# Splitting words into high and low parts: one ScalarE copy and one VectorE subtraction at every place

## The chip, the core and the metric

The kernel runs on one core of one Trainium2 chip. The metric is the device time of one execution in microseconds (us), as the median over runs. The core's engines are TensorE (PE: matmuls, with its weight loads shown apart as PEld), VectorE (DVE), ScalarE (ACT), GpSimd (POOL) and SyncE (SP), which here issues the DMAs. Each engine works through its own list of instructions in order; semaphores tie the lists together.

## What is computed

Two layers of a mixer block over 1024 latent tokens and 256 context tokens, of width 1024. Cut to what matters here:

```python
for l in range(2):
    hx = rms_norm(x, norm_g[l]) * (1 + scale) + shift        # and hc for the context
    q, k, v, g_att, c_a, c_b, g_conv, f_u, g_four = split_cols(hx @ w_in[l])
    attn = windowed_attention(rope(q), rope(k), v, kc, vc, sink)   # blocks of 128, window +-128, + 256 context keys
    y_conv = silu(layer_norm(depthwise_conv31(c_a * sigmoid(c_b))))
    y_four = real(fft2(f_u)) @ w_four + b_four
    y = concat(attn * silu(g_att), y_conv * silu(g_conv), y_four * silu(g_four)) @ w_out[l]
    x = x + gate * y                                          # layer 0 also updates the context
return rms_norm(x, final_g)
```

## The kernel before

Data are fp32. For the large products each operand is kept as two words of a shorter type, a high part and a low part: `hi` is a copy of the raw fp32 words into that type, `lo` is `raw - hi`. A product is then three matmuls, hi times hi, hi times lo and lo times hi (`mm3`, L198 to L200). Whatever goes into such a product has to be split first: one copy and one subtraction for each tile.

The order of the work is set by a scheduler that places each engine's instructions by priority with a timeline of its own; the code is written in the order of priority. Each layer runs in stages: projections beside the Fourier and convolution branches; then attention, 128 queries and two heads to a step (`Attention.step`), four steps to a block; inside attention the matmuls of other work are put as filler for TensorE, first the remaining projections (gates), then the halves of the output projection (`Out.half`). Step i computes scores of its two heads (`score`, two PSUM tiles of two banks), VectorE adds the mask and takes the row's extreme (`score<-score,mask`), ScalarE does the exponential (`p<-score,st`, L925), VectorE forms the reciprocal of the sum, GpSimd divides (`p<-p,st`, L941). A step later TensorE transposes p (L955, PSUM tile `pt`), ScalarE copies the high part (`ph`, L960), VectorE subtracts (`pl<-pt,ph`); then TensorE multiplies with v (L969, tile `mm`).

Places that split, and with which engines before:

- `w_split` (tiles `wr`, `wh`, `wl`, 128x1024): weights of the next projection; ScalarE copy (L408), subtraction on VectorE, but on GpSimd (L409) while attention runs, when `holding[0]` is true.
- `Wout.split` (tiles `wor`, `hxh`, `hxl`, 128x512, 16 in a layer): weights of the output projection, raw tiles coming through six slots that are loaded again after each split. Even k: ScalarE copy and GpSimd subtraction. Odd k: both on VectorE, the copy as a CAST.
- `Out.prep_rest` and `Out.prep` (tiles `wr`, `wh`, `wl`, 128x512): the two halves of an output block's input. The rest half goes by `holding[0]`, the other half subtracts on VectorE.
- `keys`, `w_tile_short` and the Fourier tables: ScalarE and VectorE already.

`modulate` (L400) and `four_fold` (L681, L686, L690) have subtractions of their own on GpSimd, which do not go through `split`. VectorE's instructions all have line 57, that of a recording helper, so they are told apart by their tiles.

## Time and profile before

| | |
|---|---|
| median of 3 runs | 1176.14 us (1173.57 to 1181.28) |
| the profiled execution | 1175.1 us, span of its instructions 1172.9 us |
| PE busy | 1095.1 us (93% of the span) |
| DVE busy | 828.8 us (71%) |
| ACT busy | 541.5 us (46%) |
| POOL busy | 285.7 us (24%) |
| mean granted TensorE clock | 0.972 of full speed |

Busy time is the time in which at least one instruction of the engine is on its way. What matters is the idle time of TensorE, and at which of the stages it lies. Attention runs from about 262 to 610 us in layer 0 and from about 838 to 1140 us in layer 1; the weights of the output projection are split at about 425 to 500 us and 950 to 1025 us.

### The profile page before, as it was taken

The numbers are of one execution on the slowest core, as the hardware profiler recorded it, in microseconds if no ns is written. First come the engines' busy times: TensorE is split into PE (matmuls) and PEld (weight loads), VectorE is DVE, ScalarE is ACT, GpSimd is POOL, SyncE is SP. The second block draws the span as 40 slices with busy tenths as digits, with TensorE's granted clock in tenths as the row PEclk, the third lists the DMA queues.
The fourth block names the chain that finished last, engine by engine and source line by source line (L and its number), as shares of the span: only waits on it lengthen the run. The fifth ranks groups of instructions, "written<-read, shape, count | busy, mean of one in ns | idle before, by whom it ended". The sixth has DMA issues, their size and how long they took to land.

```text
span 1172.9 us, 17178 instructions
## 1 busy us (share of the span) xinstructions
PE 1095.1 (93%) x6165; PEld 923.6 (79%) x6165; DVE 828.8 (71%) x1702; ACT 541.5 (46%) x1195; POOL 285.7 (24%) x271
## 2 busy tenths in 40 slices
PE   5999999999999999899999999989889997999986
PEld 2688887778878988788888788868678886788865
DVE  4545998997776567767665269999566677577763
ACT  4442222215566555555557653222346555455551
POOL 1230000002222234344553220000131344234321
PEclk9999999999999999899999999999989997899989
DMA  9711238453322253336458423532423254433210
GB/s 333 230 61 55 90 111 235 149 193 81 86 87 75 79 161 98 97 113 205 161 191 269 141 60 107 169 114 72 108 63 86 91 149 127 116 108 91 91 54 36
DMA packets 150924, 144.90 MB, mean 124 GB/s; under 512 B 7302, under 2 KB 128566, under 8 KB 150840
## 3 DMA queue, kind: packets, MB, share of 16 engines
q1 hardware_dynamic: 150840, 143.82, 40.5%
q8 instruction: 48, 0.79, 0.3%
q14 instruction: 36, 0.29, 0.1%
HBM read 109.71 MB, written 34.09 MB: 123 GB/s over the span
## 4 chain that ended last, share of the span: by engine, by line
PE 73%; DVE 12%; DMA 7%; ACT 3%; issue 2%; SPq 2%; POOL 1%; DVEq 0%; ACTq 0%; POOLq 0%
PE mm L198 13%; PE mm L199 13%; PE mm L200 13%; PE mm L969 5%; PE pt L955 5%; PE pt L198 5%; PE pt L199 5%; PE pt L200 4%; PE score L899 2%; PE score L901 2%; DMA wr<-od 2%; DVE score L57 2%; DVE cy L57 2%; DMA wada<-w_ada 1%; DVE pl L57 1%
## 5 line engine op out<-in xcount | busy, mean ns | idle before, releaser
L198 PE MATMUL mm<-hxh,wh 128*128 128x512 f32 (+1 forms) x808 | 312.4, 388 | 8.5 <-DVE t L57 4.5
L199 PE MATMUL mm<-hxl,wh 128*128 128x512 f32 (+1 forms) x808 | 309.4, 383 | 0.0
L200 PE MATMUL mm<-hxh,wl 128*128 128x512 f32 (+1 forms) x808 | 308.4, 382 | 0.0
L198 PEld LDWEIGHTS mm<-hxh,wh 128*128 128x128 f32 x808 | 154.2, 192 | 39.1 <-DVE t L57 5.9
L57 DVE SCALAR_TENSOR_TENSOR cy<-cu,cw,cy 128x1009 f32<-128x1009 f32 (+25 forms) x180 | 175.7, 1005 | 0.9
L200 PEld LDWEIGHTS mm<-hxh,wl 128*128 128x128 f32 x808 | 154.2, 191 | 27.6
L199 PEld LDWEIGHTS mm<-hxl,wh 128*128 128x128 f32 x808 | 154.5, 191 | 25.3 <-issue 0.5
L941 POOL TENSOR_SCALAR p<-p,st 128x640 f32<-128x640 f32 (+2 forms) x144 | 109.2, 771 | 261.9 <-DVE st L57 162.8
L57 DVE TENSOR_TENSOR pl<-pt,ph 128x512 fp32r<-128x512 f32 x184 | 111.9, 616 | 70.1 <-ACT ph L960 68.3
L409 POOL TENSOR_TENSOR wl<-wr,wh 128x512 fp32r<-128x512 f32 (+1 forms) x31 | 56.3, 1817 | 392.2 <-ACT wh L408 388.6
L960 ACT ACTIVATE ph<-pt 128x512 fp32r<-128x512 f32 x184 | 97.4, 541 | 112.4 <-PE pt L955 109.5
L925 ACT ACTIVATE p<-score,st 128x640 f32<-128x640 f32 (+2 forms) x144 | 105.5, 735 | 37.8 <-DVE st L57 36.6
L57 DVE CUSTOM_DVE_ANT_0 score<-score,mask,nsink 128x640 f32<-128x640 f32 (+2 forms) x144 | 111.1, 782 | 13.9 <-PE score L901 9.8
L408 ACT ACTIVATE wh<-wr 128x1024 fp32r<-128x1024 f32 (+1 forms) x74 | 61.8, 850 | 119.1 <-PE mm L199 72.0
L955 PE MATMUL pt<-ident,p 128*128 128x128 f32 x640 | 105.2, 283 | 11.2 <-DVE pl L57 7.8
L198 PE MATMUL pt<-hxh,wh 128*128 128x512 f32 (+1 forms) x296 | 110.7, 378 | 1.1 <-ACT gsum L341 1.1
L199 PE MATMUL pt<-hxl,wh 128*128 128x512 f32 (+1 forms) x296 | 109.4, 370 | 0.3 <-POOL hxl L400 0.3
L200 PE MATMUL pt<-hxh,wl 128*128 128x512 f32 (+1 forms) x296 | 108.3, 366 | 0.0
L969 PE MATMUL mm<-ph,v 128*128 128x256 f32 x320 | 91.5, 311 | 5.4 <-ACT ph L960 3.7
L955 PEld LDWEIGHTS pt<-ident,p 128*128 128x128 f32 x640 | 79.3, 145 | 21.9 <-issue 7.7
L969 PE MATMUL mm<-pl,v 128*128 128x256 f32 x320 | 92.9, 313 | 3.7 <-DVE pl L57 3.7
L969 PEld LDWEIGHTS mm<-ph,v 128*128 128x128 f32 x320 | 64.2, 201 | 8.9 <-ACT ph L960 5.9
(230 smaller groups left out, 1795.5 us busy)
## 6 DMA issues: line engine op xcount, KB each, us to landing
wada<-w_ada SPq DMA_DIRECT2D x48, 512.0 KB, 7.3
wr<-w_in SPq DMA_DIRECT2D x38, 512.0 KB, 4.1
qq<-qd SPq DMA_DIRECT2D x36, 256.0 KB, 4.5
x1d<-x SPq DMA_DIRECT2D x10, 512.0 KB, 3.8
xnd<-xr SPq DMA_DIRECT2D x10, 512.0 KB, 3.7
p<-xnd SPq DMA_DIRECT2D x10, 512.0 KB, 4.9
sg<-sgd SPq DMA_DIRECT2D x36, 128.0 KB, 3.0
wr<-yd SPq DMA_DIRECT2D x18, 256.0 KB, 4.3
```

Source lines behind the costliest of these rows:

```text
L57: r = f(*args, **kw)
L198: T.matmul(o, lhsT=lhs[0], rhs=rhs[0], start=start, stop=False)
L199: T.matmul(o, lhsT=lhs[0], rhs=rhs[1], start=False, stop=False)
L200: T.matmul(o, lhsT=lhs[1], rhs=rhs[0], start=False, stop=stop)
L408: S.activation(hi, raw, AF.Copy)
L409: (E or (G if holding[0] else V)).tensor_tensor(out=lo, in0=raw, in1=f32(hi), op=ALU.subtract)
L899: T.matmul(sc[:, c0:512], lhsT=q2[:, h, :], rhs=kx[:, k0:k0 + nl], start=fst, stop=not fst)
L925: S.activation(pp[:, j * n:(j + 1) * n], z["sc"][j][:, 768 - n:768], AF.Exp, scale=-1.0, bias=st[:, j:j + 1], accum_out=st[:, 4 + j:5 + j])
L941: G.tensor_scalar(out=pp[:, j * n:(j + 1) * n], in0=pp[:, j * n:(j + 1) * n], scalar1=st[:, 6 + j:7 + j], scalar2=1.0, op0=ALU.mult, op1=A ...
L955: T.transpose(out=bt[:, (j % 2 * 2 + y) * P:(j % 2 * 2 + y + 1) * P], in_=pp[:, c0:c0 + P], identity=ident)
L960: S.activation(ph, bt[:, :w], AF.Copy)
L969: T.matmul(o, lhsT=self.vv[kt][:, kv * P:(kv + 1) * P], rhs=y.cols(j * 256, (j + 1) * 256), start=(j == 0 and x == 0), stop=(j == z["nkt"] ...
```

## The change

`split` loses its arguments for engines. At each place it is now one ScalarE copy for the high part and one VectorE subtraction for the low part, inside attention too.

```diff
-    def split(hi, lo, raw, E=None, by_vector=False):
-
-        if by_vector:
-            V.tensor_copy(out=hi, in_=raw)
-        else:
-            S.activation(hi, raw, AF.Copy)
-        (E or (G if holding[0] else V)).tensor_tensor(out=lo, in0=raw, in1=f32(hi), op=ALU.subtract)
+    def split(hi, lo, raw):
+
+        S.activation(hi, raw, AF.Copy)
+        V.tensor_tensor(out=lo, in0=raw, in1=f32(hi), op=ALU.subtract)
...
-            split(self.hi[k].lat[:, hs], self.lo[k].lat[:, hs], self.raw[h, k], V if k % 2 else G, k % 2 == 1)
+            split(self.hi[k].lat[:, hs], self.lo[k].lat[:, hs], self.raw[h, k])
...
-            split(yh[:, :512], yl[:, :512], raw[:, :512], V)
+            split(yh[:, :512], yl[:, :512], raw[:, :512])
...
-                    split(kh.cols(s0, s1), kl.cols(s0, s1), raw.cols(s0, s1), V)
+                    split(kh.cols(s0, s1), kl.cols(s0, s1), raw.cols(s0, s1))
```

The scheduler places the instructions anew, so rows around the splits move too. First place: VectorE in layer 1, at the first eight splits of the output projection's weights (`hxh_6158` to `hxh_6186` are the high parts for k = 0 to 7, `wor` the raw slots, `pl_9040` the low part of p that TensorE multiplies with v, `t_9110` an evacuation that frees an `mm` bank). Before:

```order
L57 TENSOR_TENSOR ot_8878<-t_9074,mm 64x256
L57 CAST hxh_6162<-wor_9112 128x512
L57 TENSOR_TENSOR hxl_6164<-wor_9112,hxh_6162 128x512
L57 CAST hxh_6170<-wor_9113 128x512
L57 TENSOR_TENSOR hxl_6172<-wor_9113,hxh_6170 128x512
L57 CAST hxh_6178<-wor_9114 128x512
L57 TENSOR_TENSOR pl_9040<-pt,ph_9038 128x256
L57 TENSOR_TENSOR hxl_6180<-wor_9114,hxh_6178 128x512
L57 CAST hxh_6186<-wor_9112 128x512
L57 ISA score,st<-score,mask,nsink 128x640
```

Now the same place reads:

```order
L57 TENSOR_TENSOR ot_8878<-t_9074,mm 64x256
L57 ISA score,st<-score,mask,nsink 128x640
L57 ISA st 128x1
L57 TENSOR_TENSOR hxl_6160<-wor_9112,hxh_6158 128x512
L57 TENSOR_TENSOR hxl_6164<-wor_9112,hxh_6162 128x512
L57 TENSOR_TENSOR hxl_6168<-wor_9113,hxh_6166 128x512
L57 TENSOR_TENSOR hxl_6172<-wor_9113,hxh_6170 128x512
L57 TENSOR_TENSOR hxl_6176<-wor_9114,hxh_6174 128x512
L57 TENSOR_TENSOR hxl_6180<-wor_9114,hxh_6178 128x512
L57 TENSOR_TENSOR pl_9040<-pt,ph_9038 128x256
```

The mask step of the second head (the ISA row on `score`) stood behind four casts and three subtractions and now stands ahead of six subtractions.

Second place: ScalarE at the same splits (`p_9126` are the exponentials of this step's two heads). Before:

```order
L981 ACTIVATE t_9074<-mm 64x256
L408 ACTIVATE hxh_6158<-wor_9112 128x512
L933 ACTIVATE st<-nsink,st 128x1
L408 ACTIVATE hxh_6166<-wor_9113 128x512
L408 ACTIVATE hxh_6174<-wor_9114 128x512
L960 ACTIVATE ph_9038<-pt 128x256
L925 ACTIVATE p_9126,st<-score,st 128x640
L408 ACTIVATE hxh_6182<-wor_9112 128x512
L518 ACTIVATE t_9110<-mm 128x512
L925 ACTIVATE p_9126,st<-score,st 128x640
```

Now (three lines less in the file, so L405 is the copy of L408, L957 that of L960 and L922 the exponential of L925):

```order
L978 ACTIVATE t_9074<-mm 64x256
L405 ACTIVATE hxh_6158<-wor_9112 128x512
L930 ACTIVATE st<-nsink,st 128x1
L405 ACTIVATE hxh_6162<-wor_9112 128x512
L405 ACTIVATE hxh_6166<-wor_9113 128x512
L405 ACTIVATE hxh_6170<-wor_9113 128x512
L405 ACTIVATE hxh_6174<-wor_9114 128x512
L930 ACTIVATE st<-nsink,st 128x1
L405 ACTIVATE hxh_6178<-wor_9114 128x512
L957 ACTIVATE ph_9038<-pt 128x256
L922 ACTIVATE p_9126,st<-score,st 128x640 x2
```

Six copies instead of three stand ahead of `ph` and the first exponential, and none is left between the two exponentials.

Third place: VectorE in layer 0, in the first half of attention, where `w_split` makes the weights of the next projection (`t_3731` is an evacuation that frees an `mm` bank):

```order
 L57 ISA st 128x1
+L57 TENSOR_TENSOR wl<-wr,wh 128x1024
 L57 SCALAR_TENSOR_TENSOR t_3731<-t_3731,mm 128x256
 L57 ISA score,st<-score,mask,nsink 128x640
 L57 ISA st 128x1
 L57 TENSOR_TENSOR pl_3662<-pt,ph_3660 128x256
+L57 ISA score,st<-score,mask,nsink 128x640
+L57 ISA st 128x1
 L57 TENSOR_TENSOR pl_3750<-pt,ph_3748 128x512
```

The subtraction over 1024 columns now stands on VectorE, ahead of a bank's evacuation and of a mask step.

## Rows read from the trace of the kernel before

**Rows 1.** Busy time by stretch: PE, PEld, DVE, ACT, POOL, then granted clock, DMA share, GB/s.

```profile
262.00:425.00 163.00, 158.56 (x972) 140.19 (x971) 112.77 (x246) 96.15 (x227) 44.53 (x43) 1.00 0.31 85
425.00:500.00 75.00, 65.23 (x385) 58.12 (x384) 57.81 (x113) 42.13 (x100) 27.06 (x25) 0.93 0.41 119
...
950.00:1025.00 75.00, 64.10 (x324) 55.34 (x323) 53.24 (x97) 35.31 (x80) 30.35 (x25) 0.86 0.45 131
1025.00:1130.00 105.00, 99.67 (x585) 86.63 (x583) 82.12 (x209) 62.48 (x152) 38.68 (x39) 1.00 0.29 89
```

**Rows 2.** Timeline of PE: instructions with idle time before them, and releaser.

```profile
437.83 0.38 PE L969 MATMUL mm<-ph,v 128*128 128x256 f32 x1 [2.02 <-ACT ph L960]
...
472.79 0.58 PE L198 MATMUL mm<-hxh,wh 128*128 128x256 f32 x1 [2.90 <-DVE t L57]
...
968.68 0.69 PE L899 MATMUL score<-kh,q 128*128 128x384 f32 x1 [2.98 <-ACT p L925]
...
993.03 1.09 PE L955 MATMUL pt<-ident,p 128*128 128x128 f32 x4 [3.78 <-DVE pl L57]
```

**Rows 3.** Timeline of ACT around two of those waits.

```profile
436.88 0.63 ACT L408 ACTIVATE hxh<-wor 128x512 fp32r<-128x512 f32 x1 [3.93 <-DMA wor<-w_out]
...
967.74 0.79 ACT L925 ACTIVATE p<-score,st 128x640 f32<-128x640 f32 x1 [4.53 <-DVE st L57]
```

**Rows 4.** Timeline of DVE, layer 1, splits of the output projection's weights.

```profile
959.69 1.17 DVE L57 TENSOR_TENSOR hxl<-wor,hxh 128x512 fp32r<-128x512 f32 x1
960.78 0.41 DVE L57 CAST hxh<-wor 128x512 fp32r<-128x512 f32 x1
...
962.24 1.51 DVE L57 CAST hxh<-wor 128x512 fp32r<-128x512 f32 x1
...
965.37 1.48 DVE L57 CAST hxh<-wor 128x512 fp32r<-128x512 f32 x1
...
968.85 0.16 DVE L57 TENSOR_TENSOR st<-st 128x2 f32<-128x2 f32 x1
968.92 0.68 DVE L57 SCALAR_TENSOR_TENSOR cy<-cy,t 128x512 f32<-128x512 f32 x1
...
980.08 1.22 DVE L57 TENSOR_TENSOR q<-qq,q 64x1024 fp32r<-64x1024 f32 x1
...
984.01 1.79 DVE L57 SCALAR_TENSOR_TENSOR cy<-cy,t 128x512 f32<-128x512 f32 x1
985.73 1.24 DVE L57 TENSOR_TENSOR st<-st 128x2 f32<-128x2 f32 x1
...
993.74 2.19 DVE L57 TENSOR_TENSOR q<-qq,q 64x1024 fp32r<-64x1024 f32 x1
```

**Rows 5.** Timeline of POOL at the same time.

```profile
961.75 4.82 POOL L409 TENSOR_TENSOR hxl<-wor,hxh 128x512 fp32r<-128x512 f32 x3
```

**Rows 6.** Timeline of DVE, layer 0, the same splits.

```profile
432.64 2.35 DVE L57 CAST hxh<-wor 128x512 fp32r<-128x512 f32 x2
...
466.95 1.85 DVE L57 CAST hxh<-wor 128x512 fp32r<-128x512 f32 x2
```

**Rows 7.** Groups of POOL instructions that the change removes.

```profile
L409 POOL TENSOR_TENSOR wl<-wr,wh 128x1024 fp32r<-128x1024 f32 x14 | 33.4, 2386 | 353.2 <-ACT wh L408 353.2
L409 POOL TENSOR_TENSOR hxl<-wor,hxh 128x512 fp32r<-128x512 f32 x16 | 23.7, 1496 | 22.4 <-ACT hxh L408 22.3
L409 POOL TENSOR_TENSOR wl<-wr,wh 128x512 fp32r<-128x512 f32 x17 | 22.9, 1349 | 39.0 <-ACT wh L408 35.4 <-DVE wl L57 3.6
```

**Rows 8.** Groups of DVE instructions of the same kinds.

```profile
L57 DVE CAST hxh<-wor 128x512 fp32r<-128x512 f32 x16 | 12.7, 804 | 1.1 <-DMA wor<-w_out 1.0
...
L57 DVE TENSOR_TENSOR dft<-dft,dfth 128x1024 fp32r<-128x1024 f32 x8 | 9.8, 1221 | 3.0 <-ACT dfth L408 3.0
...
L57 DVE TENSOR_TENSOR hxl<-t,hxh 128x512 fp32r<-128x512 f32 x12 | 8.3, 692 | 0.4
```

**Rows 9.** Group of ACT instructions that the change doubles.

```profile
L408 ACT ACTIVATE hxh<-wor 128x512 fp32r<-128x512 f32 x16 | 10.0, 627 | 11.1 <-DMA wor<-w_out 6.6 <-PE mm L200 4.5
```

## Prediction

> **What bounds the kernel now.** I read first the table of busy time by stretch. In the first half of layer 0's attention TensorE is busy 158.6 of 163 us and VectorE 112.8 (69%): TensorE sets the pace, the others have room. In the two stretches in which the output projection's weights are split it is otherwise: TensorE is busy 65.2 of 75 us and 64.1 of 75 us, idle for 9.8 and 10.9 us, and the granted clock falls to 0.93 and 0.86 of full speed, which by these means costs another 75 x 0.07 = 5.3 us and 75 x 0.14 = 10.5 us of speed [rows 1]. So these 150 us hold 20.7 us of idle time and 15.8 us of slowness; a change that touches the splits is decided here first.
>
> Then the timeline of TensorE in these stretches, for what ended each idle time. Four waits hold 11.7 of the 20.7 us: 2.02 us for the copy `ph`, 2.90 us for an evacuation `t` of a matmul bank by VectorE, 2.98 us for an exponential that frees a score bank, 3.78 us for a `pl` subtraction that frees a transpose bank [rows 2]. One step further back, on ScalarE: the exponential of the third had waited 4.53 us for VectorE's mask step, and the `ph` of the first stood behind a weight copy that had waited 3.93 us for its w_out DMA [rows 3]. And VectorE before that mask step: a CAST of 128x512 that takes 0.41 us at 960.78 takes 1.51 us at 962.24 and 1.48 us at 965.37 [rows 4]. At that time GpSimd runs three split subtractions in a row, 4.82 us from 961.75 on [rows 5]. The same shows on other kinds of instruction, each beside its own quick copy: 1.79 against 0.68 us (`cy`), 1.24 against 0.16 us (`st`), 2.19 against 1.22 us (`q`). Together these five rows lose 1.10 + 1.07 + 1.11 + 1.08 + 0.97 = 5.3 us on VectorE in 35 us [rows 4]. In layer 0 two pairs of casts take 2.35 and 1.85 us where 0.82 would do [rows 6]. A VectorE instruction that reads its data from SBUF waits while a GpSimd subtraction is on; that is how the stretch becomes VectorE's.
>
> **The change part by part.** GpSimd loses 14 + 16 + 17 = 47 subtractions, 33.4 + 23.7 + 22.9 = 80.0 us [rows 7]. It waited for others most of the time, so nothing of this is a gain by itself.
>
> VectorE gets these 47. At undisturbed speed a 1024-column one takes 1.22 us and a 512-column one 0.69 us [rows 8]: 14 x 1.22 = 17.1 us, and 33 x 0.69 = 22.8 us. It loses 16 casts, 12.7 us with their stretching [rows 8]. That is 27 us more. Against it stands the stretching of other instructions that ends: 1.11 + 1.08 + 0.97 = 3.2 us by the rows shown, the least it can be; I take about 10 us for the whole trace as an estimate from there, since two of the six stretches of attention hold the larger part. The new subtractions can themselves meet a divide on GpSimd, which stays: one that did took 1.17 us instead of 0.69 [rows 4]. GpSimd is busy 140.6 of 418 us in the four stretches, the leaving subtractions included [rows 1], so a sixth is a fair share: 47/6 x 0.48 = 4 us, at most 23 us if all did. In all VectorE's busy time grows by some 20 us (between 14 and 40).
>
> ScalarE gets 16 copies of 0.63 us, 10.0 us in all [rows 9]; it is busy 42 and 35 of the 75 us there [rows 1].
>
> What of this lies on the path, place by place:
>
> Layer 1, first eight splits. The second mask step now stands ahead of the subtractions, so the 4.53 us wait of the exponential ends. In its place six copies stand ahead of both exponentials: 6 x 0.63 = 3.8 us. Counted from 960 us, when the first copy began, with 0.3 for a sink exponential, 0.4 for `ph` and twice 0.79 for the exponentials, the second ends at about 966.1 instead of 968.5. Saved: 2.4 of the 2.98 us.
>
> Layer 1, second eight. Ahead of the awaited `pl` the stretched `cy` and `st` give back 1.11 + 1.08 = 2.2 us; more subtractions stand there now (six for three casts and three subtractions, 4.1 for 3.3 us), which takes 0.8. Saved: 1.4 of 3.78 us.
>
> Layer 0, first eight. The copies that wait for the refilled slots now stand behind the exponentials, so `ph` does not wait for that DMA: 2.0 us saved. Layer 0, second eight: the two casts ahead of the evacuation lose 1.0 us of stretching; saved 1.0 of 2.90.
>
> Clock. In layer 1 each us of idle goes with 10.5/10.9 = 0.96 us of slowness, in layer 0 with 5.3/9.8 = 0.54. I take half of that for the us saved: 3.8 x 0.48 + 3.0 x 0.27 = 2.6 us. So far -(3.8 + 3.0 + 2.6) = -9.4 us.
>
> Cost elsewhere. The fourteen long subtractions stand in the first half of attention, ahead of evacuations and mask steps. Between 0 (VectorE has 31% idle time) and all 17.1 us. TensorE lost 4.4 us there to 112.8 us of VectorE's work [rows 1], that is 0.04 us per us; at twice that, because the new instructions stand right ahead of what TensorE awaits, 17.1 x 0.08 = 1.4 us. The seventeen short ones run mostly beside the halves of the output projection, where VectorE is at 82.1 of 105 us and TensorE loses 5.3 [rows 1]: 17 x 0.69 x 0.13 = 1.5 us. Sum: 2.9 us. The next projection's weights are ready a whole chunk of matmuls before use, so a later `wl` is covered there; without that cover it would be up to 1.22 us a time.
>
> The total is -9.4 + 2.9 = -6.5 us on an execution of 1175.1 us (span 1172.9), which is 1168.6. The median of the runs is 1 us above that execution, so I forecast **1169 us**.
>
> [...]
>
> **The rivals.** *Bigger gain.* If the lock between the two engines is what makes most of the idle time in the two stretches, since each stretched instruction delays all that stands behind it in VectorE's list, two thirds of the 20.7 us and the same part of half the 15.8 us of slowness go: -13.8 - 5.3 = -19 us, with next to no cost elsewhere: 1156 us. For it: five rows within 35 us on one engine. Against: 9 of the 20.7 us of idle time lie outside the four waits read, and `pl` and mask steps read PSUM and show no stretching.
>
> *Nothing gained.* VectorE takes on 20 us; the waits keep their length because six subtractions in one piece (4.1 us) now hold up `pl`, where casts and subtractions held it up before. The 1.4 to 2.4 us savings shrink to half and the price elsewhere doubles: -4.7 + 5.8 = +1, 1177 us.
>
> *Slower.* ScalarE's copies in front of the exponentials become what TensorE waits for. The price is 16 x 0.63 = 10.0 us, and with it half of the slowness per us of idle, some 0.5 x 10: +15 us, nothing saved: 1190 us. It decides from the point at which a block of six copies (3.8 us) plus what follows is longer than the matmuls that TensorE has in hand, some 18 of 0.23 us; the 3.93 us wait for w_out [rows 3] shows how a copy can hold ScalarE, and sixteen more of them can. Against: ScalarE's share of 47 to 56% in these stretches.
>
> The Trainium skill (Perfetto Trace Analysis, "Optimizing Scalar/DVE Operations") speaks for that side in general: where VectorE is saturated, it says, moving work to ScalarE or even GpSimd may make sense, which is what the kernel did; by it the 20 us that return to an engine busy for 71 to 78% would cost. The same section adds that moving between VectorE and GpSimd might not help, for the shared port.
>
> That the change doesn't do what it says is no rival here: no split subtraction stands in GpSimd's list any more. The subtractions of `modulate` and `four_fold` stay there, outside attention.
>
> **How the numbers follow.** The forecast case (1162 to 1176) has 0.47, the bigger gain 0.15, nothing gained (1174 to 1182) 0.19, slower 0.19. Leaving out a tenth at either end gives 1155 to 1190. About 1% is what a measurement of this kernel can tell from no change: faster than 1164.4 has the bigger gain's 0.15 and the lower edge of the forecast, 0.27 with the doubt about how rows were placed anew; slower than 1187.9 has 0.18; the rest, 0.55, lies within 1%.
>
> **What would show it.** If I am right, casts are gone from VectorE, its `cy`, `st` and `q` in the two stretches keep to 0.68, 0.16 and 1.22 us, TensorE's idle time there falls from 20.7 to about 14 us and the clock of 950 to 1025 us rises above 0.9; TensorE's busy time in the first half of attention stays above 156 of 163 us. Wrong would be: waits of TensorE for exponentials or `ph` that stand behind runs of weight copies on ScalarE; or new idle time behind `t` and mask steps, right after a `wl` of 1.22 us. Since the scheduler placed all of attention anew, a shift of a few us away from any split is possible as well, and would make the sum wrong without touching its reasons.

## Result and the profile after

| | before | after |
|---|---|---|
| median of 4 runs (us) | 1174.86 | 1158.29 |
| lowest to highest (us) | 1171.57 to 1181.28 | 1153.87 to 1159.50 |
| the profiled execution, its span (us) | 1175.1, 1172.9 | 1158.92, 1157.0 |
| mean granted clock of that execution | 0.972 | 0.980 |

The ratio of after to before is 0.984 with a 95% interval of 0.9807 to 0.9873: 18.8 us less, with 14.9 and 22.7 us at the ends of the interval; the medians differ by 16.6 us. I had forecast 1169 us, a gain of 6.5. The time lies in my range of 1155 to 1190 us and in the direction forecast, but outside the forecast case (1162 to 1176 us): the size is that of the rival I called the bigger gain (1156 us), to which I gave a chance of 0.15. Two executions at a lower granted clock, one of the kernel before at 1190.6 us and one of e10 at 1366.0 us, are left out of every ratio in this document.

The page of after, busy time by engine:

```profile
PE 1085.4 (94%) x6165; PEld 913.8 (79%) x6165; DVE 832.1 (72%) x1733; ACT 551.1 (48%) x1211; POOL 212.1 (18%) x224
```

The same line of the page before:

```profile
PE 1095.1 (93%) x6165; PEld 923.6 (79%) x6165; DVE 828.8 (71%) x1702; ACT 541.5 (46%) x1195; POOL 285.7 (24%) x271
```

These two lines divide the gain. The span fell by 15.9 us. TensorE's idle time, the span less its busy time, went from 77.8 to 71.6 us: 6.2 of it. The other 9.7 us is busy time: the same 6165 matmuls, done at a mean granted clock of 0.980 instead of 0.972, which is 23.1 us of slowness (1157.0 x 0.020) instead of 32.8 (1172.9 x 0.028). And VectorE, which got 47 subtractions and lost 16 casts (31 instructions more), is busy only 3.3 us longer; I had forecast some 20, and 14 at the least. GpSimd lost 73.6 us.

The table of busy time by stretch, after, columns as in [rows 1]:

```profile
262.00:425.00 163.00, 157.72 (x977) 140.09 (x976) 115.71 (x255) 97.78 (x230) 27.31 (x34) 1.00 0.31 83
425.00:500.00 75.00, 68.82 (x423) 60.43 (x422) 57.22 (x123) 47.04 (x110) 20.63 (x20) 1.00 0.44 133
950.00:1025.00 75.00, 68.43 (x390) 59.77 (x389) 56.88 (x121) 47.87 (x110) 18.20 (x19) 0.98 0.46 135
1025.00:1130.00 105.00, 97.43 (x554) 85.00 (x554) 79.86 (x208) 58.03 (x140) 33.17 (x33) 0.93 0.27 83
```

Against [rows 1]: in the two stretches of the w_out splits TensorE is idle for 6.2 and 6.6 us instead of 9.8 and 10.9, 12.8 in all where I had said about 14, and the clock is 1.00 and 0.98 instead of 0.93 and 0.86. In the first half of attention TensorE is busy 157.7 of 163 us, where it was 158.6: 0.8 us more idle time.

These stretches are fixed in time, and after the change the program is ahead by 8 us in the second and by 15 in the last (table of steps below), so the later rows don't show the same work. The 0.93 of the last stretch is not a loss: the clock falls at the last steps of attention in both kernels, before behind the end of this stretch, after inside it. The slices of 25 us that hold this fall, before and then after:

```profile
1125.00:1150.00 25.00, 21.22 (x99) 17.55 (x98) 14.04 (x35) 9.15 (x22) 6.98 (x8) 0.80 0.09 32
```

```profile
1100.00:1125.00 25.00, 18.29 (x94) 15.53 (x94) 17.89 (x58) 16.39 (x42) 5.86 (x8) 0.73 0.15 54
```

That is 25 x 0.20 = 5.0 and 25 x 0.27 = 6.8 us of slowness, 1.8 us given back.

What ended TensorE's idle time in the two stretches, from its timeline after (start, duration, instruction, idle time before it and releaser; the first splits of layer 0, and every wait above 1 us of the two stretches):

```profile
432.68 0.50 PE L198 MATMUL mm<-hxh,wh 128*128 128x512 f32 x1 [0.50 <-DVE t L57]
...
470.14 0.39 PE L198 MATMUL mm<-hxh,wh 128*128 128x256 f32 x1 [1.75 <-DVE t L57]
...
481.20 0.44 PE L896 MATMUL score<-kh,q 128*128 128x384 f32 x1 [1.14 <-ACT p L922]
...
979.05 0.63 PE L952 MATMUL pt<-ident,p 128*128 128x128 f32 x4 [1.86 <-DVE pl L57]
982.54 0.44 PE L896 MATMUL score<-kh,q 128*128 128x384 f32 x1 [1.80 <-ACT p L922]
986.20 0.44 PE L952 MATMUL pt<-ident,p 128*128 128x128 f32 x2 [1.53 <-DVE pl L57]
988.27 0.50 PE L966 MATMUL mm<-pl,v 128*128 128x256 f32 x1 [1.17 <-DVE pl L57]
```

Of the four waits of [rows 2] those of 2.02 and 2.98 us are gone, that of 2.90 for an evacuation is 1.75 long and that of 3.78 for a `pl` 1.86. Layer 1 keeps four waits in a row at its second eight splits, 6.4 us together, and three of them end with a `pl` of VectorE.

One new wait lies just ahead of the second stretch. VectorE and then TensorE, after:

```profile
940.91 1.47 DVE L57 TENSOR_TENSOR wl<-wr,wh 128x1024 fp32r<-128x1024 f32 x1 [0.59 <-ACT wh L405]
```

```profile
943.84 0.50 PE L198 MATMUL mm<-hxh,wh 128*128 128x512 f32 x1 [1.71 <-DVE t L57]
```

A moved 1024-column subtraction, 1.47 us long beside a divide of GpSimd that runs from 940.51 to 943.05, stands ahead of a mask step and of the evacuation `t` for which TensorE waits. The same comes once more 20 us earlier (1.48 us, and a wait of 1.71 at 923.91).

VectorE at the first eight splits of layer 1, timeline after:

```profile
961.07 0.89 DVE L57 CUSTOM_DVE_ANT_0 score<-score,mask,nsink 128x640 f32<-128x640 f32 x1
961.88 0.14 DVE L57 DVE_READ_ACCUMULATOR2_ANT st<- 128x1 f32 x1
961.88 0.81 DVE L57 TENSOR_TENSOR hxl<-wor,hxh 128x512 fp32r<-128x512 f32 x1
962.60 0.68 DVE L57 SCALAR_TENSOR_TENSOR cy<-cy,t 128x512 f32<-128x512 f32 x1
...
990.28 0.13 DVE L57 TENSOR_TENSOR st<-st 128x2 f32<-128x2 f32 x1
```

No casts; `cy` takes 0.68 us, `st` 0.13, a split subtraction 0.81. Between 959 and 992 us these three kinds take at most 0.68, 0.16 and 0.81 us, where in [rows 4] they took up to 1.79, 1.24 and 1.17. Of the two `q` of this stretch one takes 1.22 us and one, beside a divide of GpSimd, 1.68.

ScalarE at the first eight splits of layer 0, timeline after:

```profile
433.69 0.64 ACT L405 ACTIVATE hxh<-wor 128x512 fp32r<-128x512 f32 x1 [1.78 <-PE mm L200]
...
435.32 1.66 ACT L405 ACTIVATE hxh<-wor 128x512 fp32r<-128x512 f32 x3
...
437.07 1.14 ACT L405 ACTIVATE hxh<-wor 128x512 fp32r<-128x512 f32 x2
438.24 0.39 ACT L957 ACTIVATE ph<-pt 128x256 fp32r<-128x256 f32 x1
438.52 0.79 ACT L922 ACTIVATE p<-score,st 128x640 f32<-128x640 f32 x1
```

Six copies stand ahead of `ph` and the exponential, and none waits for its DMA; before, the copy at 436.88 waited 3.93 us for it [rows 3].

**Where in the program the gain lies.** VectorE runs one RECIPROCAL of `st` for each of the 72 attention steps of the two layers, so its start tells where attention stands. From VectorE's timeline, in us:

| RECIPROCAL | before | after | difference |
|---|---|---|---|
| 1st (first step of layer 0) | 281.28 | 282.06 | +0.8 |
| 16th | 408.07 | 407.90 | -0.2 |
| 19th | 440.52 | 432.54 | -8.0 |
| 40th (last of layer 0) | 611.80 | 604.15 | -7.7 |
| 41st (first of layer 1) | 851.57 | 843.35 | -8.2 |
| 53rd | 958.48 | 951.35 | -7.1 |
| 55th | 988.63 | 970.53 | -18.1 |
| 58th | 1016.47 | 1001.46 | -15.0 |
| 72nd (last) | 1134.34 | 1119.26 | -15.1 |

Between the 16th and the 19th, the first w_out splits of layer 0, 7.8 us are gained and kept to the end of the layer. Between the 53rd and the 58th, those of layer 1, 7.9 are gained and kept to the 72nd. Elsewhere the two executions run side by side, to within some us: the scheduler put other matmuls between the steps, so that a single step moves by several us either way (the 22nd comes 0.9 us later than before, the 55th 18.1 us earlier).

### The profile page after: what moved, and what is told of

Its sections match the earlier page's. It is cut to its first block, busy times and chain, and to the rows that moved or that the text cites. A ratio compares the mean times of both kernels' runs of the same rounds, so it can differ in the third digit from the quotient of the medians.

```text
span 1157.0 us, 17196 instructions
## 1 busy us (share of the span) xinstructions
PE 1085.4 (94%) x6165; PEld 913.8 (79%) x6165; DVE 832.1 (72%) x1733; ACT 551.1 (48%) x1211; POOL 212.1 (18%) x224
## 4 chain that ended last, share of the span: by engine, by line
PE 78%; DVE 6%; DMA 6%; ACT 5%; issue 2%; SPq 1%; POOL 1%; ACTq 0%; DVEq 0%; POOLq 0%
PE mm L198 14%; PE mm L199 14%; PE mm L200 14%; PE pt L952 5%; PE mm L966 5%; PE pt L198 5%; PE pt L199 5%; PE pt L200 5%; PE score L896 3%; PE score L898 2%; DMA wada<-w_ada 2%; ACT p L922 2%; DVE cy L57 1%; DVE wl L57 1%; DVE score L57 1%
## 5 line engine op out<-in xcount | busy, mean ns | idle before, releaser
L938 POOL TENSOR_SCALAR p<-p,st 128x640 f32<-128x640 f32 (+2 forms) x144 | 115.1, 812 | 732.2 <-DVE st L57 380.8
L957 ACT ACTIVATE ph<-pt 128x512 fp32r<-128x512 f32 x184 | 97.5, 543 | 97.7 <-PE pt L952 96.8
L57 DVE CUSTOM_DVE_ANT_0 score<-score,mask,nsink 128x640 f32<-128x640 f32 (+2 forms) x144 | 111.0, 781 | 14.7 <-PE score L898 13.8
L922 ACT ACTIVATE p<-score,st 128x640 f32<-128x640 f32 (+2 forms) x144 | 105.3, 735 | 28.6 <-DVE st L57 27.5
L405 ACT ACTIVATE wh<-wr 128x1024 fp32r<-128x1024 f32 (+1 forms) x74 | 62.0, 851 | 116.4 <-PE mm L199 76.9
L57 DVE TENSOR_TENSOR wl<-wr,wh 128x1024 fp32r<-128x1024 f32 (+1 forms) x74 | 76.7, 1041 | 44.6 <-ACT wh L405 44.5
L966 PE MATMUL mm<-pl,v 128*128 128x256 f32 x320 | 89.7, 305 | 1.2 <-DVE pl L57 1.2
L966 PE MATMUL mm<-ph,v 128*128 128x256 f32 x320 | 88.5, 304 | 0.5 <-ACT ph L957 0.3
L198 PEld LDWEIGHTS pt<-hxh,wh 128*128 128x128 f32 x296 | 55.6, 190 | 14.2 <-issue 2.4
```

The costliest lines, as they stand in the source:

```text
L57: r = f(*args, **kw)
L198: T.matmul(o, lhsT=lhs[0], rhs=rhs[0], start=start, stop=False)
L405: S.activation(hi, raw, AF.Copy)
L922: S.activation(pp[:, j * n:(j + 1) * n], z["sc"][j][:, 768 - n:768], AF.Exp, scale=-1.0, bias=st[:, j:j + 1], accum_out=st[:, 4 + j:5 + j])
L938: G.tensor_scalar(out=pp[:, j * n:(j + 1) * n], in0=pp[:, j * n:(j + 1) * n], scalar1=st[:, 6 + j:7 + j], scalar2=1.0, op0=ALU.mult, op1=A ...
L957: S.activation(ph, bt[:, :w], AF.Copy)
```

## The experiments

Three accounts of the gain had to be told apart. *Stretching*: VectorE's instructions that read SBUF stand still while GpSimd subtracts, and all behind them is late. *Casts*: VectorE is freed of 16 casts, which ScalarE takes. *Start*: the weight splits of `w_split` and `prep_rest` change where the scheduler puts the first w_out copies, and with that a wait for a DMA ends. Ratios below are to the kernel before, with 95% intervals, and the us are the ratio's part of the kernel before's median of the same comparison (1175.23, 1174.71 and 1175.47 us). "Layer 0" and "layer 1" are the us, against before, from the 1st to the 40th and from the 41st to the 72nd RECIPROCAL of the one profiled execution; they time the steps of attention and not all work around them, so they need not add up to the gain. The expectations call the first account the lock theory, and the third first the order and then the start theory.

| kernel | ratio | us | layer 0 | layer 1 |
|---|---|---|---|---|
| the change | 0.9840 [0.9807, 0.9873] | -18.8 | -8.4 | -6.9 |
| e1_wout_only | 0.9913 [0.9880, 0.9947] | -10.2 | +4.1 | -8.7 |
| e2_rest_only | 0.9987 [0.9961, 1.0013] | -1.5 | -2.7 | -0.5 |
| e3_wout_casts_kept | 0.9947 [0.9923, 0.9971] | -6.2 | +9.5 | -9.6 |
| e4_wout_copies_act | 0.9963 [0.9931, 0.9995] | -4.3 | +5.2 | -6.9 |
| e5_prep_rest_too | 0.9935 [0.9915, 0.9956] | -7.6 | +1.5 | -5.1 |
| e6_w_split_too | 0.9932 [0.9904, 0.9960] | -8.0 | -5.1 | -2.0 |
| e8_after_casts_v | 0.9888 [0.9855, 0.9921] | -13.2 | -7.2 | -3.6 |
| e9_after_even_pool | 0.9941 [0.9917, 0.9964] | -6.9 | -6.9 | +4.0 |
| e7_wout_early_loads | 0.9875 [0.9834, 0.9915] | -14.7 | +0.3 | -10.8 |
| e10_after_early_loads | 0.9958 [0.9930, 0.9985] | -4.9 | -1.1 | +2.3 |
| e11_after_even_memset | 0.9862 [0.9827, 0.9896] | -16.2 | -8.1 | -3.5 |
| e12_after_rest_v | 0.9892 [0.9855, 0.9929] | -12.7 | -6.8 | -0.4 |

**One part of the change alone.** e1 has the change in the w_out splits and nowhere else; e2 is its complement:

In e1, against before:

```diff
-            split(self.hi[k].lat[:, hs], self.lo[k].lat[:, hs], self.raw[h, k], V if k % 2 else G, k % 2 == 1)
+            split(self.hi[k].lat[:, hs], self.lo[k].lat[:, hs], self.raw[h, k], V)
```

In e2, against before:

```diff
-        (E or (G if holding[0] else V)).tensor_tensor(out=lo, in0=raw, in1=f32(hi), op=ALU.subtract)
+        (E or V).tensor_tensor(out=lo, in0=raw, in1=f32(hi), op=ALU.subtract)
```

Expected of e1:

> The kernel before, with the change made in Wout.split alone (all 16 high parts of a layer copied on ScalarE, all subtractions on VectorE); w_split and prep_rest still subtract on GpSimd inside attention. Lock theory (a GpSimd subtraction holds up VectorE's SBUF-reading instructions in the stretches where w_out is split): 11 to 15 us faster than before, the rest of the change being worth 2 to 5. Cast theory (it is the casts leaving VectorE): the same, 11 to 15 us faster. Order theory (it is where the scheduler puts the splits, which the other subtractions move by a step): 0 to 6 us faster.

Expected of e2:

> The kernel before, with the change made everywhere but in Wout.split: the 31 subtractions of w_split and prep_rest go from GpSimd to VectorE, the w_out splits stay as they were (even ones on ScalarE and GpSimd, odd ones cast and subtracted on VectorE). Lock theory and cast theory: 2 us slower to 4 us faster, VectorE's casts still stretched to 1.5 us beside GpSimd. Order theory: 6 to 14 us faster, since the splits start a step later, as in the changed kernel.

e1 gains 10.2 us, between the 0 to 6 expected from the order and the 11 to 15 from the other two accounts; e2 gains 1.5, which can't be told from none and is not the 6 to 14 expected from the order. The sum, 11.7, falls short of the change's 18.8 by some 7, with 6 either way by the three intervals (root of the sum of their squares). So the w_out splits are the larger part; the 31 subtractions of `w_split` and `prep_rest` bring nothing that can be measured alone, and probably something beside the first.

The traces show one place where the two parts meet. ScalarE's and TensorE's timelines of e1, first w_out splits of layer 0:

```profile
437.75 0.63 ACT L408 ACTIVATE hxh<-wor 128x512 fp32r<-128x512 f32 x1 [3.18 <-DMA wor<-w_out]
```

```profile
438.70 0.39 PE L969 MATMUL mm<-ph,v 128*128 128x256 f32 x1 [3.15 <-ACT ph L960]
```

e1 keeps the wait of `ph` behind a copy that waits for its DMA, and it is longer here than before, 3.15 us for 2.02 [rows 2]. e2 has lost this wait and gains 7.7 us between the 16th and the 19th RECIPROCAL, as the change does, but gives 6.0 of them back by the 26th, where it still has the casts and GpSimd's subtractions. In layer 1 it comes to the 58th RECIPROCAL 8.7 us sooner after the 53rd than before, with w_out splits as before, and loses this again later; so that the layer 1 gain is due to these splits rests on the times of e1 and e2, and not on the steps. TensorE's timeline of e2:

```profile
443.81 0.79 PE L198 MATMUL mm<-hxh,wh 128*128 128x512 f32 x1 [2.57 <-DVE t L57]
...
469.73 0.63 PE L955 MATMUL pt<-ident,p 128*128 128x128 f32 x4 [1.63 <-DVE pl L57]
```

**The w_out splits taken apart.** e3 takes GpSimd out of them and leaves the odd casts on VectorE; e4 gives all copies to ScalarE and leaves GpSimd its half of the subtractions. Both start from before:

In e3, against before:

```diff
-            split(self.hi[k].lat[:, hs], self.lo[k].lat[:, hs], self.raw[h, k], V if k % 2 else G, k % 2 == 1)
+            split(self.hi[k].lat[:, hs], self.lo[k].lat[:, hs], self.raw[h, k], V, k % 2 == 1)
```

In e4, against before:

```diff
-            split(self.hi[k].lat[:, hs], self.lo[k].lat[:, hs], self.raw[h, k], V if k % 2 else G, k % 2 == 1)
+            split(self.hi[k].lat[:, hs], self.lo[k].lat[:, hs], self.raw[h, k], V if k % 2 else G)
```

Expected of e3:

> The kernel before, with the even w_out subtractions moved from GpSimd to VectorE, and the odd high parts still cast on VectorE: GpSimd is out of these splits, VectorE has the most work there (16 subtractions and 8 casts a layer). Lock theory: 6 to 12 us faster than before, casts 0.42 us each. Cast theory: no gain or up to 5 us slower, VectorE having 5.5 us more a layer. Order theory: within 4 us of the kernel with the change in Wout.split alone.

Expected of e4:

> The kernel before, with all 16 w_out copies of a layer on ScalarE, and the even subtractions still on GpSimd: VectorE has the least work there (8 subtractions a layer), GpSimd as much as before. Lock theory: 0 to 5 us faster, with VectorE's subtractions and cy, st and q still stretched beside GpSimd. Cast theory: 8 to 13 us faster. Order theory: within 4 us of the kernel with the change in Wout.split alone.

6.2 and 4.3 us; the sum, 10.5, is near e1's 10.2, with intervals of 3 to 4 us either way on each. Both lie where the stretching account had them (6 to 12, 0 to 5) and not where the cast account had them (no gain or slower, 8 to 13). Moving the casts alone does bring something beside GpSimd, where casts are themselves stretched; how much is not settled within these intervals.

**Which of the other splits does it.** e5 is e1 with `prep_rest` on VectorE as well, e6 is e1 with `w_split` on VectorE:

In e5, beside e1's edit:

```diff
-                split(yh[:, 512:], yl[:, 512:], raw[:, 512:])
+                split(yh[:, 512:], yl[:, 512:], raw[:, 512:], V)
```

In e6, beside e1's edit:

```diff
-        split(wh, wl, raw)
+        split(wh, wl, raw, V)
```

Expected of e5:

> The change in Wout.split and in prep_rest, while w_split's fourteen long subtractions stay on GpSimd inside attention. In its order of instructions layer 0's first w_out copy still stands behind the same exponentials as before the change. Start theory (w_split's move lets the w_out splits of layer 0 begin one attention step later, after their DMA has landed): as the kernel with the change in Wout.split alone, 8 to 13 us faster than before, with ScalarE waiting some 3 us for w_out in layer 0. Load theory (each subtraction that leaves GpSimd gives its own share): 12 to 16 us faster.

Expected of e6:

> The change in Wout.split and in w_split, while prep_rest's seventeen short subtractions stay on GpSimd inside attention. In its order layer 0's first w_out copy stands one step later, as in the changed kernel. Start theory: as the changed kernel within 4 us, 13 to 19 us faster than before, and no wait of ScalarE for w_out over 1 us in layer 0. Load theory: 9 to 13 us faster, since only part of the other subtractions moved.

In time both are e1 again (7.6 and 8.0 us against 10.2, intervals overlapping): neither makes up the missing 7 us by itself. By time e6 is a miss of the start account, which wanted 13 to 19 us, and neither reaches what its expectation gave for a share of each subtraction that moves (12 to 16 for e5, 9 to 13 for e6). In the trace they differ as the start account says. ScalarE of e5 still waits 4.01 us for a w_out DMA, and TensorE 3.92 behind it; e6 has neither: TensorE's one wait there between 426 and 450 us is 0.79 us, for an evacuation of VectorE.

Over all kernels the layer 0 column divides by `w_split`: with its subtractions on VectorE (the change, e2, e6, e8 to e12) layer 0 is 1.1 to 8.4 us shorter than before, without (e1, e3, e4, e5, e7) 0.3 to 9.5 us longer. What e6 wins in layer 0 it lacks in layer 1, where it gains 2.0 us for e1's 8.7. Its executions also spread from 1160.8 to 1174.7 us, so one profiled execution says little about that.

**The casts and GpSimd, from the changed kernel.** e8 gives the odd casts of the w_out splits back to VectorE; e9 gives the even subtractions back to GpSimd, which takes them from VectorE; e11 gives GpSimd, in place of these subtractions, three writes of zeros each, so it leaves out the low parts of the even w_out blocks:

In e8, against the changed kernel:

```diff
-            split(self.hi[k].lat[:, hs], self.lo[k].lat[:, hs], self.raw[h, k])
+            if k % 2:
+                V.tensor_copy(out=self.hi[k].lat[:, hs], in_=self.raw[h, k])
+                V.tensor_tensor(out=self.lo[k].lat[:, hs], in0=self.raw[h, k], in1=f32(self.hi[k].lat[:, hs]), op=ALU.subtract)
+            else:
+                split(self.hi[k].lat[:, hs], self.lo[k].lat[:, hs], self.raw[h, k])
```

In e9:

```diff
+            if k % 2 == 0:
+                S.activation(self.hi[k].lat[:, hs], self.raw[h, k], AF.Copy)
+                G.tensor_tensor(out=self.lo[k].lat[:, hs], in0=self.raw[h, k], in1=f32(self.hi[k].lat[:, hs]), op=ALU.subtract)
+            else:
...
```

In e11:

```diff
+            if k % 2 == 0:
+                S.activation(self.hi[k].lat[:, hs], self.raw[h, k], AF.Copy)
+                for _ in range(3):
+                    G.memset(f32(self.lo[k].lat[:, hs]), 0.0)
+            else:
...
```

Expected of e8:

> The changed kernel with the odd w_out high parts cast on VectorE again; nothing of the splits on GpSimd. Lock theory: casts take 0.42 us each and the kernel stays 12 to 17 us faster than the one before, up to 5 us slower than the changed kernel for 6.7 us more of VectorE's time. Cast theory (VectorE's work is what counts): 6 us or more slower than the changed kernel.

Expected of e9:

> The changed kernel with the even w_out subtractions on GpSimd again, all copies on ScalarE. Lock theory: VectorE's subtractions, cy, st and q beside them are stretched again, and 4 to 10 us of the gain go back. Cast theory: within 3 us of the changed kernel, or faster by as much, since VectorE has 11 us less to do.

Expected of e11:

> The changed kernel with the even w_out subtractions replaced by three GpSimd memsets of the low part each, which write SBUF and read none of it; the low parts of these weight blocks, and so a part of the correction terms, are left out. GpSimd is busy there as with its subtractions. Lock theory (what hurts is GpSimd reading SBUF beside VectorE): 14 to 22 us faster than before, VectorE's cy, st, q and subtractions at their undisturbed 0.68, 0.16, 1.22 and 0.69 us. Rival (GpSimd being slow and in the way of its own divides): 5 to 9 us faster, as with the subtractions on GpSimd.

e9 falls back to -6.9 us, about 12 us worse than the change, with intervals that don't touch, though VectorE has sixteen subtractions fewer; the lock theory had 4 to 10, the cast theory 3 at most. e11 keeps the gain: -16.2, its interval clear of e9's, where the lock theory had 14 to 22 and its rival 5 to 9. GpSimd's share of the w_out splits, e9 and e11:

```profile
L1065 POOL TENSOR_TENSOR hxl<-wor,hxh 128x512 fp32r<-128x512 f32 x16 | 23.9, 1499 | 22.9 <-ACT hxh L1064 15.0 <-DMA wr<-od 7.6
```

```profile
L1066 POOL MEMSET hxl<- 128x512 f32 x48 | 23.5, 528 | 18.4 <-PE mm L199 17.7
```

GpSimd is as busy with the one as with the other, 23.9 and 23.5 us. VectorE runs 1717 instructions in both kernels, and not as fast. From the pages of e9 and of e11:

```profile
PE 1087.8 (94%) x6165; PEld 914.8 (79%) x6165; DVE 835.0 (72%) x1717; ACT 551.6 (47%) x1211; POOL 234.8 (20%) x240
```

```profile
PE 1085.4 (94%) x6165; PEld 913.0 (79%) x6165; DVE 822.8 (71%) x1717; ACT 551.7 (48%) x1211; POOL 230.8 (20%) x272
```

That is 12.2 us more for the same kinds and numbers of instructions beside a GpSimd that reads, and more than the change's 832.1 for a list of 1733. The groups of VectorE in e9 and in e11 show on which instructions:

```profile
L57 DVE TENSOR_TENSOR hxl<-wor,hxh 128x512 fp32r<-128x512 f32 x16 | 16.7, 1071 | 0.3 <-ACT hxh L405 0.3
...
L57 DVE TENSOR_TENSOR st<-st 128x2 f32<-128x2 f32 x72 | 13.6, 188 | 19.0 <-ACT st L930 9.7 <-ACT p L922 9.1
L57 DVE SCALAR_TENSOR_TENSOR wr<-wr,sg 128x512 f32<-128x512 f32 x15 | 12.8, 853 | 10.9 <-DMA wr<-od 10.6 <-issue 0.4
L57 DVE RECIPROCAL st<-st 128x2 f32<-128x2 f32 x72 | 11.8, 164 | 1.7
```

```profile
L57 DVE TENSOR_TENSOR st<-st 128x2 f32<-128x2 f32 x72 | 11.8, 164 | 20.3 <-ACT p L922 11.7 <-ACT st L930 8.3
L57 DVE RECIPROCAL st<-st 128x2 f32<-128x2 f32 x72 | 11.7, 162 | 1.5
L57 DVE TENSOR_TENSOR hxl<-wor,hxh 128x512 fp32r<-128x512 f32 x16 | 11.6, 737 | 1.6 <-ACT hxh L405 1.6
L57 DVE SCALAR_TENSOR_TENSOR wr<-wr,sg 128x512 f32<-128x512 f32 x15 | 10.8, 722 | 13.7 <-DMA wr<-od 10.5 <-issue 3.0 <-DVE pl L57 0.2
```

The kinds that read two operands from SBUF (`hxl`, `st`, `wr`) take 1071, 188 and 853 ns beside the subtractions, 737, 164 and 722 beside the writes; RECIPROCAL, which reads one, stays at 162 to 164 in both. The two timelines of e9 over one stretch show single cases, GpSimd first:

```profile
458.54 2.99 POOL L1065 TENSOR_TENSOR hxl<-wor,hxh 128x512 fp32r<-128x512 f32 x2 [7.63 <-DMA wr<-od]
...
464.01 1.28 POOL L1065 TENSOR_TENSOR hxl<-wor,hxh 128x512 fp32r<-128x512 f32 x1
```

```profile
459.01 1.37 DVE L57 SCALAR_TENSOR_TENSOR wr<-wr,sg 128x512 f32<-128x512 f32 x1
...
464.45 0.86 DVE L57 TENSOR_TENSOR st<-st 128x2 f32<-128x2 f32 x1 [0.26 <-ACT p L922]
...
465.43 0.69 DVE L57 TENSOR_TENSOR hxl<-wor,hxh 128x512 fp32r<-128x512 f32 x1
```

The comparison can be made one by one, since the writes of e11 don't wait for the copies and need not lie where the subtractions of e9 do. Of VectorE's instructions that overlap in time with a write, ten `hxl` take 0.70 us in the mean, four `st` 0.16 and two `wr` 0.69; of those that overlap with a subtraction in e9, nine `hxl` take 1.32, two `st` 0.75 and two `wr` 1.50. Instructions whose second operand is in PSUM don't change beside a subtraction: five `pl` of 512 columns take 0.68 us, and those without one 0.69. That the split comes later from GpSimd is not it either: no wait of TensorE in e9 ends with a GpSimd subtraction of w_out, and no wait of ScalarE with a w_out DMA. TensorE's waits for GpSimd's divides are 2.5 us in e9 and 1.0 in e11, so GpSimd in the way of its own divides can be 1.5 us.

So the stretching account holds in the changed order: GpSimd's reads beside VectorE's two-input instructions, not GpSimd's occupation, lengthen VectorE's list and go with the loss of time. The Trainium skill (SBUF — State Buffer, "Who interferes with whom") says just this, that a VectorE instruction with two SBUF inputs contends with a GpSimd instruction that reads SBUF and not with one that only writes; 1071 against 737 ns agrees. Two inputs are not the whole of it: a cast reads one operand, and of the sixteen before, nine that overlap with a GpSimd subtraction take 1.11 us in the mean and the other seven 0.42. No run here shows what sets it apart from RECIPROCAL. The loss shows in the steps of layer 1, which take 10.9 us longer in e9 than in the change (+4.0 against -6.9); the two profiled executions as a whole differ by 6.0 us.

e8 costs little: -13.2 us, its interval overlapping with the change's, and within the 12 to 17 us of the stretching account. In the changed order the casts are worth between nothing and about 6 us; without GpSimd's subtractions beside them they are short, 0.44 us in the mean instead of 0.80 before.

**The w_out loads.** If the wait for the w_out DMA is what e1 lacks, loading earlier should bring it. e7 (from e1) and e10 (from the change) issue the six first w_out loads one projection sooner:

```diff
+            for _ in range(6):
+                wo.load()
             raw = w_begin(l, C_GC + P)
...
-            for _ in range(6):
-                wo.load()
```

Expected of e7:

> The kernel with the change in Wout.split alone, and the first six w_out loads issued one projection earlier; w_split and prep_rest subtract on GpSimd as before the change. Start theory (in layer 0 it is the w_out DMA, met too early, that takes back what the split's engines give): 13 to 18 us faster than the kernel before, ScalarE's wait for w_out in layer 0 gone, and the steps there as early as in the changed kernel. Rival (w_split's own engine counts, not the DMA): 8 to 12 us, as without the early loads.

Expected of e10:

> The changed kernel with the first six w_out loads issued one projection earlier. Start theory: within 4 us of the changed kernel, which starts its splits after the loads have landed; 15 to 22 us faster than before. Rival: if loads still hold something up, 3 to 6 us faster than the changed kernel.

e7 gains 14.7 us: in its trace the wait of `ph` is gone (one of 2.71 us for a `pl` came 7 us later), and it wins 6.4 us between the 16th and the 19th RECIPROCAL where e1 lost 1.0. This bears the start account out at its place, though not what in it acts: with the earlier loads the scheduler also put the first copies later in the order of the work, at 438.33 us, right ahead of the 19th RECIPROCAL (438.95), where in e1 they begin 12 us ahead of it (429.30 and 441.30). By time it is within the 13 to 18 us expected, and 4.5 us better than e1 with overlapping intervals, so likely and not sure. e10 went the other way, against both expectations: it has 4.9 us left of 18.8, with intervals well apart. ScalarE and TensorE of e10:

```profile
428.88 1.06 ACT L870 ACTIVATE q<-qq 128x1024 fp32r<-128x1024 f32 x1 [4.14 <-DMA od<-ot]
```

```profile
430.75 0.38 PE L966 MATMUL mm<-ph,v 128*128 128x256 f32 x1 [1.60 <-ACT ph L957]
```

Another copy on ScalarE now waits for a DMA, and `ph` stands behind it as it stood behind the w_out copy before. This wait is 1.6 of the some 14 us on TensorE; what makes the rest is open.

**Further along the same way.** e12 takes the change's idea to the remaining subtractions on GpSimd, those of `modulate` and `four_fold`, outside attention:

```diff
-            E = G if k % 4 == 3 else V
+            E = V
...
-            G.tensor_tensor(out=el[:, q], in0=e, in1=f32(eh[:, q]), op=ALU.subtract)
+            V.tensor_tensor(out=el[:, q], in0=e, in1=f32(eh[:, q]), op=ALU.subtract)
...
```

Expected of e12:

> The changed kernel with the 22 split subtractions of modulate and four_fold moved from GpSimd to VectorE as well. Lock theory: up to 4 us faster than the changed kernel, since VectorE's instructions between 625 and 700 us are no longer stretched by some 4 us. Load theory: same or up to 4 us slower, VectorE being the busier engine at the start of the layers.

-12.7 us, not better than the change and probably worse, by more than the 4 us that its expectation allowed. VectorE's busy time rises to 842.7 us there. No kernel tried beats the change; e11 and e7 come within the intervals.

## Why the prediction was right, and where its sizes were off

**The place.** Right. Both gains of the table of steps lie at the w_out splits, and e1 shows that a change there alone brings 10.2 us.

**What VectorE's instructions do beside GpSimd.** Right as a mechanism, shown by e9 against e11; too wide as a rule, since the prediction had every VectorE instruction wait that reads its data from SBUF, and RECIPROCAL, which does, stays at 0.15 to 0.16 us beside a subtraction, before and in e9. Mis-sized as a term: "I take about 10 us for the whole trace". The rows of after give the real value. From the groups of VectorE after:

```profile
L57 DVE TENSOR_TENSOR wl<-wr,wh 128x1024 fp32r<-128x1024 f32 x38 | 47.7, 1254 | 41.3 <-ACT wh L405 41.3
...
L57 DVE TENSOR_TENSOR wl<-wr,wh 128x512 fp32r<-128x512 f32 x36 | 29.1, 816 | 3.3 <-ACT wh L405 3.3
...
L57 DVE TENSOR_TENSOR hxl<-wor,hxh 128x512 fp32r<-128x512 f32 x32 | 21.7, 724 | 0.1
```

and before, where three groups answer to them:

```profile
L57 DVE TENSOR_TENSOR wl<-wr,wh 128x1024 fp32r<-128x1024 f32 x24 | 29.4, 1224 | 23.3 <-ACT wh L408 23.3
...
L57 DVE TENSOR_TENSOR wl<-wr,wh 128x512 fp32r<-128x512 f32 x19 | 16.6, 875 | 8.0 <-ACT wh L408 7.3 <-PE mm L969 0.7
...
L57 DVE TENSOR_TENSOR hxl<-wor,hxh 128x512 fp32r<-128x512 f32 x16 | 13.2, 839 | 0.2
```

These groups grew by 18.3 + 12.5 + 8.5 = 39.3 us and the casts [rows 8] took 12.7 with them: +26.6, where I had 27 and 4 more for meeting divides. All groups of VectorE together grew by 6.8 us (its busy time, which counts overlaps once, by 3.3), so everything else on it got some 20 us shorter, not 10. The upper bound of 40 us for VectorE's growth doesn't follow from its own terms either, which give 27 - 3.2 + 23 = 47. The five rows of [rows 4] already held 5.3 us in 35; I should have counted such instructions over the trace, not guessed from one stretch.

**The savings place by place.** Right in sum: I had 6.8 us less idle time in the two stretches, and 7.9 came (20.7 to 12.8); with the new wait of 1.71 us just ahead of the second one it is 6.2. By TensorE's timeline, layer 1 saved 4.3 us (waits of 10.8 us in all before, 6.6 after) for the 3.8 forecast; layer 0 saved 3.2 at the first eight splits (3.7 to 0.5) for 2.0, and 0.2 at the second eight (5.7 to 5.5) for 1.0, since new waits of 0.3 to 1.1 us took the place of the one that got shorter. The reason given for layer 0, copies behind the exponentials, was right but not whole: without the change in `w_split` the wait for the w_out DMA stays (e1, e5), with it or with earlier loads it goes from ahead of `ph` (e6, e7).

**The clock.** This is the term that was mis-sized most: "I take half of that for the us saved", 2.6 us. Over the whole span TensorE's busy time fell by 9.7 us for the same matmuls. That is 7.1 of the 9.4 us by which the profiled execution gained more than the 6.5 forecast; idle time makes the other 2.3 (6.2 us for 6.8 - 2.9 = 3.9). In the two stretches the slowness went from 15.8 us to 75 x 0.02 = 1.5, nearly all of it, 1.8 us were given back at the last steps of attention, and some 3 us more elsewhere. Where it went shows best at the first splits of layer 0. The table by stretch, before (the clock is the last column but two):

```profile
425.00:450.00 25.00, 21.18 (x115) 18.07 (x114) 18.98 (x37) 12.91 (x30) 8.63 (x8) 0.93 0.61 185
```

and after:

```profile
425.00:450.00 25.00, 24.50 (x145) 21.42 (x144) 18.23 (x41) 15.81 (x38) 6.11 (x6) 1.00 0.63 197
```

Idle time fell by 3.3 us here and the granted clock is 1.00 throughout, the 2.4 GHz level, which is 25 x 0.07 = 1.8 us more by the means of the prediction. That makes 5.1 of the 7.8 us between the 16th and the 19th RECIPROCAL; the other 2.7 are not located, since the scheduler placed other matmuls between these steps. A price per us of idle time was the wrong form: over all of 425 to 500 us the clock is 1.00 with 6.2 us idle of 75, and from 1100 to 1125 it is 0.73 with 6.7 us idle of 25.

**Cost elsewhere.** Forecast 2.9 us. TensorE's idle time fell by 6.2 us in all and by 7.9 in the two stretches, so 1.7 us came elsewhere in the balance. It is not where I looked first: the 1st and the 16th RECIPROCAL lie about 1 us closer together than before, so the long subtractions in the first half of layer 0's attention cost at most the 0.8 us of idle time more that TensorE has there. In layer 1's attention my own sign of being wrong came, new idle time behind `t` right after a `wl`: two waits of 1.71 us, each behind one that a divide had stretched to 1.5 us. I had priced the meeting with divides on VectorE and not on TensorE.

**The rivals.** The slower one did not come: TensorE's waits for exponentials rose from 14.7 to 19.3 us over the trace, a balance of 4.6 us more, of which the copies can be a part, where 10 to 15 were feared; one of them, 1.80 us at 982.54, does stand behind two weight copies and a `ph` on ScalarE. The bigger gain, by the lock, which is VectorE's waiting beside a GpSimd subtraction, came out at its size. It had 0.15 because 9 of 20.7 us of idle time lay outside the waits I had read; that doubt was sound for idle time and left out the clock. This rival was right in its total, by luck, two errors of opposite sign, and wrong in its split: it claimed 13.8 us of idle time and 5.3 of clock, and 6.2 and 9.7 came over the whole span.

**Open.** Why the parts together bring more than their sum, if they do; why e10 loses 14 us; and why e6, with layer 0 as quick as the change's, is no faster than e1. Each edit makes the scheduler place all of attention anew, and the layer 1 column differs by 6.5 us between the change and e12, which have the same splits there.

## What to carry to other kernels

Where VectorE and GpSimd both read SBUF, count what VectorE's short instructions lose beside GpSimd before taking GpSimd's time as free: here 80 us of subtractions taken from GpSimd made VectorE busy only 3.3 us longer. Look for it in one group's shortest and longest copies (0.41 and 1.51 us for the same CAST), then add up over the whole trace. And when TensorE's idle time shrinks, allow for most of the clock that goes with it (14.3 of 15.8 us in the two stretches here), not for half. Compare stretches by their place in the program: a stretch fixed in time showed a loss of clock in the last one that was the same fall, come 15 us sooner.

## What was unexpected

Executions of one kernel differ with the granted clock. Those of e2 range from 1167.3 us at 0.985 to 1181.7 us at 0.966, which is 14.4 us for 0.019, or 7.6 us for each 0.01; those of before, in the first comparison of the experiments, from 1168.1 at 0.979 to 1182.9 at 0.968. The four executions of after have 0.980 to 0.989, these 28 of before 0.966 to 0.982. The clock, which makes the larger part of the gain, is so also what varies from execution to execution, and the intervals are 0.2 to 0.4% either way.

A 128x2 `st` instruction, 0.13 us by itself, took 0.86 us in e9 and 1.24 us before [rows 4]: for their length the shortest instructions lose most. Both end within 0.03 us of the end of the GpSimd subtraction beside them (465.29 us in e9, 986.95 before): they wait it out.
